# S5 lag table in DRAM with lags outside groups, its transfers on GpSimd's queue, output products issued strip by strip

## The chip, the cores and the metric

The kernel runs on one core of one Trainium2 chip, as one launch. The metric is the device time of the whole launch in microseconds (us). The engines that matter here: PE (TensorE, matrix products), PEld (its weight loads), DVE (VectorE), ACT (ScalarE), POOL (GpSimd) and SP (SyncE, which only issues DMAs). DMAs are issued from the queues of SP, ACT and POOL and are carried out by 16 DMA engines.

## The reference, cut to what matters

Two layers over 256 tokens of 2048 features: an S5 layer with its MLP, then a differential-attention layer with its MLP. The change touches the S5 mixer only. It has 128 groups of 16 features, and each group has 64 complex states:

```python
def s5_mixer(x, w_in, a_re, a_im, log_dt, b_re, b_im, c_re, c_im, d_skip, w_glu):
    u = (x @ w_in).reshape(Bsz, L, SSM_GROUPS, SSM_GROUP)
    step = exp(log_dt)[:, None]
    lam_re, lam_im = minimum(a_re, -1e-4), a_im
    abar = exp(step * lam_re) * (cos, sin)(step * lam_im)
    bbar = (abar - 1) / lam * b                       # complex
    # per group g: s_t = abar_g s_{t-1} + bbar_g u_t ;  y_t = Re(c_g s_t)
    y = y + d_skip * u
    z = gelu(y)
    val, gate = split(z @ w_glu)
    return val * sigmoid(gate)
```

Whatever way the recurrence is cut, y is a sum over earlier tokens of a 16x16 matrix that depends on the group and on the lag only, plus what a state carries over from further back.

## The kernel before, in words

**Chunks of eight tokens.** The 256 tokens are cut into 32 chunks of 8. Inside a chunk, y is a product with a Toeplitz operand built from the lags 0 to 7; what comes from earlier chunks goes through the states at the chunks' borders. The 128 groups are worked in 8 units of 16 groups (`unit(hh)`, called unit 0 to 7 here). A unit runs in four steps:

1. Lines 606 to 615: A (powers of abar) and B are loaded by POOL, DVE makes E from them (lines 609 to 612), and PE sums each chunk's input into the states (L615, bank `psw`).
2. Lines 621 to 648: cb is loaded by POOL, DVE makes F (lines 627 to 629), and PE makes the lag table (L634, bank `psk`). ACT copies it to K (L642), DVE adds d_skip on the diagonal (L643), and four DMAs write K to the scratch `k_scr` in DRAM (L645). Eight DMAs then read it back as M (L648), one for each token of a chunk: each lands on 16 partitions, shifted by one lag against the one ahead, which is how the table becomes the Toeplitz operand. Slots 0 to 6 of `k_scr` hold zeros, which line 537 writes at the start.
3. Lines 652 to 683: the states are transposed (L657), turned by tables that POOL loads (rt, L660), scanned over the chunks on DVE and written to ST (L682, L683).
4. Lines 685 to 699: the output products. For each of 16 groups PE multiplies Vh with M (L690) and adds ST times F (L691) in the same piece of the bank `psy`; then DVE transposes (L694) and ACT applies the GELU. Units 0 to 3 write z32, units 4 to 7 the tile xa.

PE's array is used there in column strips: a group's product has 32 output partitions, and `tile_position=(0, 32 * g4)` names one of four strips. Line 689 walks the groups in order, two for each strip.

**What stands beside the units.** Two matrix products give PE work that does not belong to a unit: x @ w_in (L581, 16 chunks of weights, 1 MB each, 16 products of 128x512 in the trace for each) and the first 10 chunks of w_glu (L210, 32 products of 128x256 in the trace for each), which need z32 of units 0 to 3. The string `ORDER` says in which order the program's text issues pieces of x @ w_in (W) and steps of the units (digits). The framework's scheduler then makes one fixed order for each engine out of it; each engine works through its order and waits wherever an operand is not there. The weights (`raw`) have two buffers, and SP issues their loads as the buffers come free.

**Queues.** SP issues the weights, and in the kernel before also K's writes and M's reads. POOL issues A, B, cb and rt. After the units come the rest of w_glu (L187, L188, with weights split in two parts by ACT and DVE at lines 137 and 138), the MLP, the attention layer and its MLP, which the change leaves alone.

In the order lists below, `mb` is a bank of PE's results for a unit, `gb` one of the weight products, and numbers in names only count tiles.

Of the kernel before, what the change touches and what calls it, by code (L numbers as in the profile page):

```python
# [42 lines left out]
def trunk(tc, io, stop=None):  # L43
# [47 lines left out]
    class Slots:  # L91
        """the pools that a kind of buffer is drawn from in turn"""
# [19 lines left out]
    fine = [0]  # so many of the next weight blocks are split in short steps  # L112

    pinned = []  # what the splits of the next weight blocks queue behind
# [31 lines left out]
    class Moving:  # L146
        """16 feature tiles of [x hi | x lo], kept as two tiles"""
# [17 lines left out]
    def gemm_b(jobs, x, kts, group=1, tail=1):  # L165
        """jobs: (lazy weight chunk, evacuation); each makes one tile of 128 output features x 256 tokens
        from weights hi/lo and [x hi | x lo]. The last jobs sum all three products in one half of the
        bank, the others keep hi*hi apart from the two cross products."""
# [23 lines left out]
    def added(acc, out, other=None):  # L192
        """out = what the bank holds (+ other)"""
# [24 lines left out]
    class SumSq:  # L218
        """sum of squares over all features: the last term joins on the tensor engine"""
# [23 lines left out]
    class SumSqPE:  # L243
        """the same, every term on the tensor engine, four column tiles side by side"""
# [22 lines left out]
    def rstd_of(sums):  # L267
        """1 / sqrt(sums * scale + eps)"""
        ps, scale = sums
        sd = tmp("n1", bufs=1, pool_=late["p"])  # L270
        S.activation(sd, ps, AF.Sqrt, bias=eps, scale=scale)
        r = tmp("rst", bufs=2, pool_=late["p"])
        V.reciprocal(r, sd)
        return r
# [9 lines left out]
    def finish(gpost, r):  # L284
        """out = h + rms(y)*gpost, where the tensor engine adds the first tiles"""
# [17 lines left out]
    def post_norm(ss, gpost, outs):  # L303
        """h += rms(y)*gpost ; then for every tile the next norms' inputs: outs = [(dst, gpre)]"""
# [18 lines left out]
    # ------------------------------------------------------------------ S5 layer  # L323
    def s5():
# [9 lines left out]
        k_scr = dr.tile([G, SG, 15, SG], F32, name="k_scr")  # L334
# [18 lines left out]
        # ---- x*g, with the first weights between its parts  # L353
# [17 lines left out]
        # ---- tables in [group, state]  # L371
# [26 lines left out]
        # sin/cos of th through the half angle  # L398
# [24 lines left out]
        # powers of abar: pw[:, delta, ri, n]  # L423
# [25 lines left out]
        # coef = (abar - 1) / lam, B = abar^delta * coef kept as (Br, -Bi, -Br)  # L449
# [32 lines left out]
        # u^8 (unit) and mag^8, doubled over both partition halves  # L482
# [26 lines left out]
        # chunk rotations e^{i phi c}  # L509
# [24 lines left out]
        # zero slots of the lag table, D on its diagonal  # L534
        zt = ps_.tile([P, SG * 7 * SG], F32, name="zt")
        V.memset(zt, 0.0)
        DMA.dma_start(k_scr[:, :, 0:7, :], zt.rearrange("g (p s q) -> g p s q", p=SG, q=SG))
# [8 lines left out]
        # ---- per 16 groups  # L546
# [47 lines left out]
        def unit(hh):  # L594
# [6 lines left out]
            for jj in range(2):  # L601
# [11 lines left out]
                for g in range(8):  # L613
# [24 lines left out]
            # lag table -> DRAM -> Toeplitz operand  # L638
            K = ut("K", [4, 8, SG], bufs=2)
            for c4 in range(4):  # L640
                q = slice(32 * c4, 32 * c4 + 16)
                S.copy(K[q], psk[q].rearrange("p (s d q) -> p s d q", s=4, q=SG))  # L642
                V.tensor_tensor(K[q, :, 0, :], K[q, :, 0, :], dskip[q, 4 * hh : 4 * hh + 4, :], op=ADD)  # L643
                k0 = k_scr[0, 0, 0, 0:1]
                DMA.dma_start(dview(k0, (g0 + c4) * 3840 + 7 * SG, [[240, 16], [4 * 3840, 4], [1, 128]]), K[q].rearrange("p s d q -> p s (d q)"))  # L645
            M = ut("M", [16, 8 * SG], bufs=2)
            for t_ in range(8):
                DMA.dma_start(M[16 * t_ : 16 * t_ + 16], dview(k_scr[0, 0, 0, 0:1], g0 * 3840 + t_ * SG, [[240, 16], [3840, 16], [1, 128]]))  # L648
# [492 lines left out]
```

## Time and profile before

| | us |
|---|---|
| median of 3 runs | 2409.82 |
| lowest, highest | 2400.21, 2413.78 |
| the profiled execution, its span from first to last instruction | 2406.2 |
| PE busy | 2274.4 (95% of the span) |
| DVE busy | 1567.2 |
| ACT busy | 1000.6 |
| POOL busy | 30.4 |

The page's slices of 60.2 us show where PE is not full: its first seven tenths read 7 7 5 7 6 8 9, all later ones 9 or 8. The S5 units lie in slices 2 to 6. For the profiled execution only its span is given, and no time around it.

### The profile page before, as it was taken

Reading aid. Unit: us, or ns where it says so; the run is one execution under the profiler, and the core shown is the slowest. Engines: PE = TensorE matmul, PEld = TensorE weight load, DVE = VectorE, ACT = ScalarE, POOL = GpSimd, SP = SyncE. Lnnn points to the kernel's source line nnn. Section 1 sums busy time; section 2 is a strip of 40 time slices with the busy share of each in tenths; the row PEclk is TensorE's granted clock in tenths of the full one; section 3 lists DMA queues with packets and bytes.
Section 4 is the critical chain, followed back from the end, with each engine's and each line's share of the span. In section 5 each row is a group of like instructions: output and inputs, shape, how many; then the busy total and the mean of one; then the engine's idle time right before and its main releaser. Section 6 shows DMA issues by size and latency. Waiting matters only on the chain.

```text
span 2406.2 us, 32521 instructions
## 1 busy us (share of the span) xinstructions
PE 2274.4 (95%) x13137; PEld 1903.0 (79%) x13137; DVE 1567.2 (65%) x2392; ACT 1000.6 (42%) x1470; POOL 30.4 (1%) x54
## 2 busy tenths in 40 slices
PE   7757689989999999999999999998999999999999
PEld 3335578868888888888868888886888888888887
DVE  8557656867556656656668896656765665665655
ACT  3011125554444444443554455444544444444442
POOL 0100100000000000000000000000000000000000
PEclk9878889999999999999999999999999999999999
DMA  9888976425554554554525544443555555555542
GB/s 282 198 167 159 165 172 248 174 97 210 201 202 173 197 191 174 197 190 158 206 99 188 180 171 162 158 175 123 189 197 210 181 187 192 183 186 192 186 165 104
DMA packets 93943, 432.25 MB, mean 180 GB/s; under 512 B 17377, under 2 KB 39649, under 8 KB 46433
## 3 DMA queue, kind: packets, MB, share of 16 engines
q1 hardware_dynamic: 82624, 405.51, 50.5%
q0 software_dynamic: 9984, 22.04, 4.8%
q10 hardware_dynamic: 1184, 2.62, 0.3%
q8 instruction: 103, 1.69, 0.3%
q14 instruction: 48, 0.39, 0.0%
HBM read 423.44 MB, written 6.68 MB: 179 GB/s over the span
## 4 chain that ended last, share of the span: by engine, by line
PE 85%; DMA 8%; DVE 4%; SPq 1%; ACT 1%; issue 1%; DVEq 0%; ACTq 0%
PE gb L187 47%; PE gb L188 24%; DMA M<-k_scr 4%; DMA raw<-in_w_in_dram 2%; PE gb L184 2%; PE gb L183 2%; PE gb L185 2%; PE mb L256 1%; PE gb L581 1%; DMA k_scr<-K 1%; PE gb L959 1%; PE gb L957 1%; PE gb L958 1%; SPq L648 1%; PE mb L690 1%
## 5 line engine op out<-in xcount | busy, mean ns | idle before, releaser
L138 DVE TENSOR_TENSOR wlo<-raw,whi 128x2048 fp32r<-128x2048 f32 (+1 forms) x540 | 803.1, 1506 | 509.8 <-ACT whi L137 507.6
L137 ACT CAST whi<-raw 128x2048 fp32r<-128x2048 f32 (+1 forms) x540 | 673.3, 1278 | 573.9 <-PE gb L187 375.1
L187 PE MATMUL gb<-x,whi 128*128 128x512 f32 x2400 | 848.8, 398 | 0.0
L188 PE MATMUL gb<-x,wlo 128*128 128x256 f32 x2400 | 675.1, 281 | 0.0
L187 PEld LDWEIGHTS gb<-x,whi 128*128 128x128 f32 x2400 | 450.6, 188 | 109.6
L187 PE MATMUL gb<-xa,whi 128*128 128x512 f32 x1296 | 465.2, 398 | 0.0
L188 PEld LDWEIGHTS gb<-x,wlo 128*128 128x128 f32 x2400 | 453.0, 189 | 0.2
L187 PE MATMUL gb<-xb,whi 128*128 128x512 f32 x1176 | 419.5, 395 | 0.4 <-ACT whi L137 0.4
L188 PE MATMUL gb<-xa,wlo 128*128 128x256 f32 x1296 | 367.8, 284 | 0.0
L188 PE MATMUL gb<-xb,wlo 128*128 128x256 f32 x1176 | 332.0, 283 | 1.6 <-DVE wlo L138 1.6
L187 PEld LDWEIGHTS gb<-xa,whi 128*128 128x128 f32 x1296 | 244.7, 189 | 61.9 <-issue 2.0
L187 PEld LDWEIGHTS gb<-xb,whi 128*128 128x128 f32 x1176 | 221.4, 188 | 52.8 <-issue 2.5
L188 PEld LDWEIGHTS gb<-xa,wlo 128*128 128x128 f32 x1296 | 245.7, 190 | 8.5 <-issue 8.2
L188 PEld LDWEIGHTS gb<-xb,wlo 128*128 128x128 f32 x1176 | 222.9, 190 | 5.2 <-issue 2.9
L215 ACT COPY cr<-gb 128x256 f32<-128x256 f32 x323 | 118.3, 368 | 169.1 <-PE gb L188 167.2
L581 PE MATMUL gb<-raw,h 128*128 128x512 f32 x256 | 122.3, 634 | 23.7 <-DMA raw<-in_w_in_dram 15.6
L162 ACT CAST x<-t 128x256 fp32r<-128x256 f32 x128 | 51.8, 406 | 198.9 <-DVE t L791 174.5
L581 PEld LDWEIGHTS gb<-raw,h 128*128 128x128 f32 x256 | 50.3, 202 | 88.3 <-issue 62.5
L690 PE MATMUL mb<-M,Vb 128*32 128x128 f32 x256 | 36.0, 338 | 76.0 <-DMA M<-k_scr 63.4
L200 DVE TENSOR_TENSOR t<-gb,cr 128x256 f32<-128x256 f32 x151 | 63.1, 418 | 54.9 <-ACT cr L215 54.5
L690 PEld LDWEIGHTS mb<-M,Vb 128*32 128x32 f32 x256 | 19.9, 130 | 82.1 <-issue 78.5
L210 PE MATMUL gb<-z,raw 128*128 128x256 f32 x320 | 72.3, 387 | 2.6 <-DMA raw<-in_w_glu_dram 2.6
(272 smaller groups left out, 2058.5 us busy)
## 6 DMA issues: line engine op xcount, KB each, us to landing
raw<-in_w_up_dram SPq DMA_DIRECT2D x128, 1024.0 KB, 4.7
raw<-in_w_down_dram SPq DMA_DIRECT2D x128, 1024.0 KB, 4.7
raw<-in_w_glu_dram SPq DMA_DIRECT2D x32, 1024.0 KB, 5.1
raw<-in_w_k_dram SPq DMA_DIRECT2D x16, 1024.0 KB, 4.7
raw<-in_w_q_dram SPq DMA_DIRECT2D x16, 1024.0 KB, 4.7
raw<-in_w_v_dram SPq DMA_DIRECT2D x16, 1024.0 KB, 4.7
raw<-in_w_o_dram SPq DMA_DIRECT2D x16, 1024.0 KB, 4.7
raw<-in_w_in_dram SPq DMA_DIRECT2D x15, 1024.0 KB, 10.8
```

What stands on the lines that cost most here:

```text
L137: S.copy(hi[:, c : c + n], raw[:, c : c + n])
L138: V.tensor_tensor(lo[:, c : c + n], raw[:, c : c + n], hi[:, c : c + n].bitcast(F32), op=SUB)
L162: mark[0] = S.copy(dst.hi(dt), src)
L183: T.matmul(ps[:, 0:L], hi[:, c], x.hi(kt), start=f, stop=False)
L184: T.matmul(ps[:, 0:L], hi[:, c], x.lo(kt), start=False, stop=False)
L187: T.matmul(ps, hi[:, c], x.both(kt), start=f, stop=False)
L188: T.matmul(ps[:, L : 2 * L], lo[:, c], x.hi(kt), start=False, stop=l)
L200: V.tensor_tensor(out, ps[:, 0:L], cr, op=ADD)
L210: T.matmul(ps[:, 0:L], w[:, off + kt * P : off + kt * P + P], x[:, kt, :], start=(kt == 0), stop=(kt == nk - 1))
L215: S.copy(cr, ps[:, L : 2 * L])
L581: T.matmul(pss[e], xg[:, kt, e * P : e * P + P], w[:, k4 * 512 : k4 * 512 + 512], start=(kt == 0), stop=(kt == 15))
L690: T.matmul(o, Vh[:, 8 * jj + g, :], M[:, 8 * jj + g, :], start=True, stop=False, tile_position=(0, 32 * g4))
```

## The change

`k_scr` is laid out anew. Before it was [group, feature, lag slot, feature], so that one group's 8 lags of a row are 512 bytes in one run. Now it is [unit, c4, feature, lag slot, 4 groups x 16 features]: four groups of a unit lie beside each other inside a lag, so that 8 lags of a row and four groups are 2 KB in one run. K and M take the matching shapes, and M is read by PE with a stride between lags. The zeros are written in 512 runs of 1792 bytes instead of 2048 of 448. K's writes and M's reads go out on POOL's queue instead of SP's. The input sums (L615) walk the strips 0, 1, 2, 3 in turn, and the output products come as four products with M, one for each strip, and then four with ST.

```diff
-        k_scr = dr.tile([G, SG, 15, SG], F32, name="k_scr")
+        k_scr = dr.tile([8, 4, SG, 15, 4 * SG], F32, name="k_scr")
...
-        zt = ps_.tile([P, SG * 7 * SG], F32, name="zt")
+        zt = ps_.tile([P, 4, 7 * 4 * SG], F32, name="zt")
         V.memset(zt, 0.0)
-        DMA.dma_start(k_scr[:, :, 0:7, :], zt.rearrange("g (p s q) -> g p s q", p=SG, q=SG))
+        DMA.dma_start(dview(k_scr[0, 0, 0, 0, 0:1], 0, [[4 * 960, P], [960, 4], [1, 448]]), zt)
...
-                for g in range(8):
+                for g in (0, 2, 4, 6, 1, 3, 5, 7):
                     g4, gh = g // 2, g % 2
...
-            K = ut("K", [4, 8, SG], bufs=2)
+            K = ut("K", [8, 4, SG], bufs=2)
+            k0 = k_scr[0, 0, 0, 0, 0:1]
             for c4 in range(4):
                 q = slice(32 * c4, 32 * c4 + 16)
-                S.copy(K[q], psk[q].rearrange("p (s d q) -> p s d q", s=4, q=SG))
-                V.tensor_tensor(K[q, :, 0, :], K[q, :, 0, :], dskip[q, 4 * hh : 4 * hh + 4, :], op=ADD)
-                k0 = k_scr[0, 0, 0, 0:1]
-                DMA.dma_start(dview(k0, (g0 + c4) * 3840 + 7 * SG, [[240, 16], [4 * 3840, 4], [1, 128]]), K[q].rearrange("p s d q -> p s (d q)"))
-            M = ut("M", [16, 8 * SG], bufs=2)
+                S.copy(K[q], psk[q].rearrange("p (s d q) -> p d s q", s=4, q=SG))
+                V.tensor_tensor(K[q, 0, :, :], K[q, 0, :, :], dskip[q, 4 * hh : 4 * hh + 4, :], op=ADD)
+                nc.gpsimd.dma_start(dview(k0, (4 * hh + c4) * 15360 + 448, [[960, 16], [1, 512]]), K[q].rearrange("p d s q -> p (d s q)"))
+            M = ut("M", [4, 8, 4, SG], bufs=2)
             for t_ in range(8):
-                DMA.dma_start(M[16 * t_ : 16 * t_ + 16], dview(k_scr[0, 0, 0, 0:1], g0 * 3840 + t_ * SG, [[240, 16], [3840, 16], [1, 128]]))
+                nc.gpsimd.dma_start(
+                    M[16 * t_ : 16 * t_ + 16].rearrange("p c t s q -> p c (t s q)"),
+                    dview(k0, 4 * hh * 15360 + t_ * 64, [[960, 16], [15360, 4], [1, 512]]),
+                )
...
             for jj in range(2):
-                for g in range(8):
-                    g4, gh = g // 2, g % 2
-                    o = psy[32 * g4 : 32 * g4 + 32, (2 * jj + gh) * P : (2 * jj + gh) * P + P]
-                    T.matmul(o, Vh[:, 8 * jj + g, :], M[:, 8 * jj + g, :], start=True, stop=False, tile_position=(0, 32 * g4))
-                    T.matmul(o, ST[:, jj, gh, g4, :], Fs[jj][:, g, 1:9, :].rearrange("p d q -> p (d q)"), start=False, stop=True, tile_position=(0, 32 * g4))
+                for gh in range(2):
+                    outs = [psy[32 * i : 32 * i + 32, (2 * jj + gh) * P : (2 * jj + gh) * P + P] for i in range(4)]
+                    for g4 in range(4):
+                        gl = 8 * jj + 2 * g4 + gh
+                        T.matmul(outs[g4], Vh[:, gl, :], M[:, gl % 4, :, gl // 4, :], start=True, stop=False, tile_position=(0, 32 * g4))
+                    for g4 in range(4):
+                        f = Fs[jj][:, 2 * g4 + gh, 1:9, :].rearrange("p d q -> p (d q)")
+                        T.matmul(outs[g4], ST[:, jj, gh, g4, :], f, start=False, stop=True, tile_position=(0, 32 * g4))
```

The scheduler makes another order out of this. On PE, at the last two units, the order before has unit 7's sums, lag table and transposes, then two chunks of w_glu (raw_1974, raw_1996), and then unit 7's output products, bank mb_1765:

```order
L615 MATMUL mb_1655<-E_1661,Vb_1283 32x128 x8
L615 MATMUL mb_1655<-E_1678,Vb_1283 32x128 x8
L634 MATMUL mb_1656<-F_1693,cb_1691 16x128 x8
L634 MATMUL mb_1656<-F_1706,cb_1691 16x128 x8
L657 MATMUL mb_1743<-ident,wsb_1741 128x128 x4
L210 MATMUL gb_1976<-z_406,raw_1974 128x256 x8
L210 MATMUL gb_1986<-z_406,raw_1974 128x256 x8
L210 MATMUL gb_1998<-z_406,raw_1996 128x256 x8
L210 MATMUL gb_2008<-z_406,raw_1996 128x256 x8
L690 MATMUL mb_1765<-M_1732,Vb_1283 32x128
```

The order of the change at the same place on PE:

```order
L615 MATMUL mb_1655<-E_1661,Vb_1283 32x128 x8
L615 MATMUL mb_1655<-E_1678,Vb_1283 32x128 x8
L634 MATMUL mb_1656<-F_1693,cb_1691 16x128 x8
L634 MATMUL mb_1656<-F_1706,cb_1691 16x128 x8
L660 MATMUL mb_1743<-ident,wsb_1741 128x128 x4
L694 MATMUL mb_1765<-M_1732,Vb_1283 32x128 x4
L697 MATMUL mb_1765<-F_1693,STt_413 32x128 x4
```

No weight product stands any more between unit 7's lag table and its output products; it is the same for unit 6, and all ten chunks of w_glu now stand ahead of unit 5's output products.

On PE, at unit 2 (bank mb_702 is its lag table, mb_991 its output), the order of the change:

```order
L634 MATMUL mb_702<-F_850,cb_848 16x128 x8
L634 MATMUL mb_702<-F_863,cb_848 16x128 x8
L660 MATMUL mb_900<-ident,wsb_898 128x128 x4
L615 MATMUL mb_945<-E_951,Vb_660 32x128 x8
L615 MATMUL mb_945<-E_968,Vb_660 32x128 x8
L210 MATMUL gb_1822<-z_406,raw_1820 128x256 x2
L210 MATMUL gb_1832<-z_406,raw_1820 128x256 x2
L210 MATMUL gb_1844<-z_406,raw_1842 128x256 x2
L210 MATMUL gb_1854<-z_406,raw_1842 128x256 x2
L694 MATMUL mb_991<-M_889,Vb_660 32x128 x4
```

Before, two whole chunks of w_in (raw_1167 and raw_1213) stood between unit 2's lag table and its output products; now it is two quarters of a w_glu chunk, and the w_in chunks have moved ahead of unit 1's output products. Unit 3 stands in the same way.

On POOL, at unit 4 (K_1251, M_1264), one piece of the difference:

```order
 L621 DMA cb_1540<-in_cb_dram 128x768
+L645 DMA k_scr<-K_1251 16x512 x4
 L606 DMA A_1506<-a_scr 128x1x1024
-L660 DMA rt_1597<-rot_scr 128x2x256
+L648 DMA M_1264<-k_scr 16x4x512 x8
 L607 DMA B_1507<-in_bE_dram 128x1x1024
 L606 DMA A_1523<-a_scr 128x1x1024
 L607 DMA B_1524<-in_bE_dram 128x1x1024
+L663 DMA rt_1597<-rot_scr 128x2x256
```

K's four writes and M's eight reads now stand on POOL between the loads for unit 6 (A_1506 to B_1524) and the tables for later units; on SP only weights are left.

Counted over the S5 part, weight chunks that PE works between a unit's lag table and its output products (w_in chunks for units 0 to 2 or 3, w_glu chunks for the later ones; a chunk of either takes PE about as long):

| unit | 0 | 1 | 2 | 3 | 4 | 5 | 6 | 7 | after 7 |
|---|---|---|---|---|---|---|---|---|---|
| before | 2.75 | 2 | 2 | 1.75 | 2.25 | 2 | 2 | 2 | 1 |
| change | 5 | 3.1 | 0.5 | 0.5 | 4.3 | 4.2 | 0 | 0 | 0 |

## Rows read from the trace of the kernel before

**Rows 1.** The page, part 1: busy us (share of the span), instructions.
```profile
PE 2274.4 (95%) x13137; PEld 1903.0 (79%) x13137; DVE 1567.2 (65%) x2392; ACT 1000.6 (42%) x1470; POOL 30.4 (1%) x54
```

**Rows 2.** Waits, 0 to 420 us: total us, times, longest.
```profile
PE mb L690 <- DMA M<-k_scr: 63.4, 6, 23.0
...
PE mb L690 <- issue: 11.6, 1, 11.6
```

**Rows 3.** PE in order of time: start us, us, what, [idle before <- releaser].
```profile
88.05 19.19 PE L581 MATMUL gb<-raw,h 128*128 128x512 f32 x44
119.27 0.60 PE L690 MATMUL mb<-M,Vb 128*32 128x128 f32 x2 [12.03 <-DMA M<-k_scr]
...
135.46 7.03 PE L581 MATMUL gb<-raw,h 128*128 128x512 f32 x16
...
173.87 0.61 PE L690 MATMUL mb<-M,Vb 128*32 128x128 f32 x2 [23.00 <-DMA M<-k_scr]
...
310.40 0.66 PE L657 MATMUL mb<-ident,wsb 128*128 128x128 f32 x4
...
328.52 0.60 PE L690 MATMUL mb<-M,Vb 128*32 128x128 f32 x2 [3.65 <-DMA M<-k_scr]
...
335.05 0.79 PE L615 MATMUL mb<-E,Vb 128*32 128x128 f32 x20
...
335.93 1.12 PE L634 MATMUL mb<-F,cb 128*16 128x128 f32 x23
337.37 0.65 PE L657 MATMUL mb<-ident,wsb 128*128 128x128 f32 x4 [0.32 <-ACT wsb L652]
337.86 13.98 PE L210 MATMUL gb<-z,raw 128*128 128x256 f32 x64
353.42 0.38 PE L690 MATMUL mb<-M,Vb 128*32 128x128 f32 x2 [1.58 <-DMA M<-k_scr]
...
357.65 7.17 PE L210 MATMUL gb<-z,raw 128*128 128x256 f32 x32
...
367.56 0.39 PE L188 MATMUL gb<-xb,wlo 128*128 128x256 f32 x1 [1.59 <-DVE wlo L138]
```

**Rows 4.** The chain that ended last, 0 to 420 us: start us, us, what.
```profile
151.66 21.88 DMA M<-k_scr
...
315.50 1.63 DMA k_scr<-K
...
340.81 1.60 DMA k_scr<-K
...
346.09 7.19 DMA M<-k_scr
```

**Rows 5.** Tile M: its reads on SP (ns min/median/max) and their landing.
```profile
L648 SPq DMA_DIRECT2D M<-k_scr x64: 302/448/2357, 94.1 to 346.1; - x64
...
DMA to landing us min/median/max: 3.0/7.4/21.9
```

**Rows 6.** Tile cb: its loads on POOL (ns min/median/max) and their landing.
```profile
L621 POOL DMA_DIRECT2D cb<-in_cb_dram x8: 557/578/616, 25.3 to 276.8; - x8
...
DMA to landing us min/median/max: 3.5/8.4/29.1
```

**Rows 7.** Tile A: its loads on POOL and their landing.
```profile
L606 POOL DMA_DIRECT2D A<-a_scr x16: 576/602/724, 22.9 to 291.4; - x16
...
DMA to landing us min/median/max: 6.4/15.0/28.2
```

**Rows 8.** DMA issues, 0 to 400 us: count, KB each, median us to landing.
```profile
raw<-in_w_glu_dram SPq DMA_DIRECT2D x22, 1024.0 KB, 7.4
raw<-in_w_in_dram SPq DMA_DIRECT2D x15, 1024.0 KB, 10.8
```

**Rows 9.** All engines in order of time, unit 6's last write to ST on DVE.
```profile
320.98 0.41 DVE L683 TENSOR_TENSOR STt<-t,t 64x248 f32<-64x248 f32 x1
```

**Rows 10.** One window: us, PE, PEld, DVE, ACT, POOL busy (count), PEclk, DMA share, GB/s.
```profile
160.00:200.00 40.00, 23.86 (x186) 14.47 (x188) 21.92 (x31) 4.13 (x7) 3.71 (x6) 0.79 1.00 170
```

## The prediction

> **What bounds the kernel now.** I read the busy times first: PE is busy 95% of the span [rows 1], so little is to be had outside the stretch where it is not full, the S5 units. There I read what PE waits for. The longest wait is for M, the lag table read back from DRAM: 63.4 us in six waits, and one of 11.6 us at the same line is put down to "issue" [rows 2]; together 75.0 us ahead of output products. In order of time the pattern is plain: PE works its weight chunks to 107.24 (88.05 + 19.19), then idles 12.0 us for unit 0's M, 23.0 for unit 1's, and at the end 3.7 for unit 6's and 1.6 for unit 7's [rows 3]. The chain says why: M's last read lands 21.9 us after its issue in unit 1 and 7.2 in unit 7 [rows 4]; over all 64 reads the landing is 3.0 at best, 7.4 in the middle [rows 5]. In 160 to 200 us the DMA engines are fully busy at only 170 GB/s, and PE's mean granted clock is 0.79: part of the stretch runs at 1.2 GHz instead of 2.4 [rows 10]. So the stage is bound by K's and M's trip through DRAM, unit after unit, less the weight chunks that PE has meanwhile.
>
> That trip, from the end of a unit's transposes (L657) to its first output product, is 15.4 us in unit 7 (338.02 to 353.42) and 17.5 in unit 6 (311.06 to 328.52) [rows 3], with two chunks of 7.0 us each as cover. The change shortens the trip, but it also takes the cover away from units 2, 3, 6 and 7 and gives it to units 0, 1, 4 and 5. The sum has to weigh both.
>
> **The change part by part.** I sum the stretch from 107.24, up to where both orders are nearly alike, to 367.56, where the split weight products run (L188). It lasts 260.3 us before. The order on PE behind it is the same.
>
> *Work that only moves.* Six w_in chunks at 7.03 are 42.2; ten w_glu chunks at 13.98 / 2 = 6.99 are 69.9 [rows 3]. A unit's sums, table and transposes take 3.0 (335.05 to 338.02) [rows 3]; what lies in the stretch, seven units less what runs inside a trip, is 19.9.
>
> *Strip by strip.* Unit 7's 64 output products take 4.2 us (353.42 to 357.65), 66 ns each, and unit 6's, after a wait, 6.5 (328.52 to 335.05) [rows 3]. No row shows products with M and ST alternating over strips. The nearest are the table's products, which change strips each time (1.12 / 23 = 49 ns), and the sums (0.79 / 20 = 40 ns) [rows 3]. I take 45 ns: 2.9 us at the full clock and 2.9 x 6.5 / 4.2 = 4.4 after a wait. Bounds: no gain at all, and 40 ns. M's strided read on PE has no row either; I take nothing for it, and the no-gain bound covers a loss. Four units with cover and four without: 4 x 2.9 + 4 x 4.4 = 29.2.
>
> *The trip.* In unit 7 K's last write is issued 2.8 us after the transposes (340.81) and lands after 1.6; eight reads follow, and the last lands 7.2 after its issue [rows 4]. On POOL's queue: 2.8 stays. The landing of a 32 KB write there has no row; it lies between 1.6 on SP's queue and 3.5, the quickest 384 KB load on POOL's [rows 6], and I take 2.3, nearer to the small transfer. An issue on POOL costs 0.58 [rows 6], so eight are 4.6. With a quarter of the runs and no weights loading beside it, the last 128 KB should land in the best time seen, 3.0 [rows 5]; the other bound is 7.2, as now. Sum 12.7. In unit 6 ACT and DVE have unit 5's results to handle first, and K's last write goes out 4.4 after the transposes (315.50) [rows 4]: 14.3. The trip can't be shorter than ST, which is written 10.3 after unit 6's transposes [rows 9, 3].
>
> *Waits for M afterwards.* Units 0, 1, 4, 5 have 5, 3.1, 4.3 and 4.2 chunks, about 22 us or more, and hide a trip even if a load of A stands ahead of M in POOL's queue (unit 4: M's eighth read waits for A_1506's semaphore, 15.0 us at the median [rows 7]). That cover is gone only if M needs over 22 us. Unit 2 has unit 3's sums and half a chunk, 4.5 us; unit 3 half a chunk, 3.5; units 6 and 7 nothing. Waits: 12.7 - 4.5 = 8.2, 12.7 - 3.5 = 9.2, 14.3 and 12.7, together 44.4, where it was 75.0.
>
> *What is late next: weights.* PE takes more chunks in a row, and two buffers allow one load ahead. With 10.8 us for a w_in load and 7.4 for a w_glu load [rows 8], each issued as the chunk two ahead is done: 3.9 at the first chunk (its buffer is free after 28 of the 44 products from 88.05 on, at 100.3 [rows 3]), 3.8 at the third, 3.8 at the fifth and sixth, 5.6 at the second w_glu chunk, a quarter of which stands ahead of unit 1's output, and 5.7 at the third, whose buffer is free only after unit 3. With 1.3 for E of unit 2, 24.1. Without K's and M's short runs on SP's queue loads may land sooner: if each takes 7.4, some 12 us of this go.
>
> *POOL's queue.* Twelve more issues a unit, 7 us, on an engine that is busy 30 us in all [rows 1]. Behind them wait the loads of A and B for later units and rt; DVE needs them only after the next output products, 15 us or more later, and I cost that at nothing; if that cover fails, E comes late by the excess. The zeros in longer runs and their place on SP's queue ahead of the first big loads lie before 107.24; nothing there waits for them by the rows, so nothing.
>
> *Tail.* From unit 7's last product to the split weights it is 9.9 us (357.65 to 367.56), of which a w_glu chunk fills 7.2 now [rows 3]. That chunk has moved ahead; the 9.9 stand bare.
>
> Sum: 42.2 + 69.9 + 19.9 + 29.2 + 44.4 + 24.1 + 9.9 = 239.6, against 260.3: a gain of 20.7 us. The profiled execution's span is 2406.2, nothing is given around it, and the median of the runs lies 3.6 higher. 2406.2 - 20.7 + 3.6 = 2389.
>
> **The rivals.** *Strips don't overlap*: products accumulating in one place, M then ST, keep 66 ns. For it speaks that today's order, where two neighbouring pairs also change strips, shows none of the sums' 40 ns. Units lose 1.3 and 2.1 each, 4 x 1.3 + 4 x 2.1 = 13.6: 2403.
>
> *The landing stays*: bytes, not runs, set it, and the last read lands after 7.2. Four bare trips grow by 4.2: 2406. Against it: fully busy DMA engines at 170 GB/s [rows 10] speak of costly short runs.
>
> *Cover lost, slower than before*: K and M queue behind A, B and cb on POOL's queue, where A's median landing is 15.0 [rows 7]. If the bare trips' reads land like that, each grows by 12.0: 48 us, 2437. It decides from a landing of 3.0 + 20.7 / 4 = 8.2 us on (no gain), and 11.2 makes it slower by over 0.5%. For it: units 2 and 3 have those loads near. Against it: units 6 and 7 have none ahead that is not long landed.
>
> *DVE holds up POOL's issues*: each of twelve issues waits for the DVE instruction that is running, 21.92 / 31 = 0.71 us [rows 10]. Four bare trips grow by 8.5: 34 us, 2423. Against it, the issues on POOL span only 557 to 616 and 576 to 724 ns [rows 6, 7] while DVE is busy over half the time. The Trainium skill has this as a rule against moving DMAs to that queue ("SBUF — State Buffer", SBUF: two separate sides): descriptors of GpSimd's DMAs can't be written while a DVE instruction in a two-port mode holds the shared port, and one took 3100 ns instead of 620. By that figure twelve issues could lose 30 us a unit, an estimate from that page of the Trainium skill; the trace's issues show no such case, so it stays at a small chance.
>
> The change may also fail to do what it says in the first place: the reads may not get cheaper (the landing rival) or the strips not overlap (the first).
>
> **How the numbers follow.** Forecast, with loads and trips somewhat better or worse: 0.66. Strips 0.11, landing 0.09, cover lost 0.10, DVE 0.04. On the good side, all loads at 7.4 give -12 (2377), and trips at ST's bound -11 (2366). The range 2366 to 2412 takes in the forecast, the strips and the landing, and leaves out cover lost, DVE and a little below. A measurement of this kernel can tell about 0.5%, 12 us: faster is below 2398, slower above 2422. Faster: the forecast and a third of the strips' case, 0.69. Same: the rest of the strips, the landing and a part of DVE, 0.18. Slower: 0.13.
>
> **What would show it.** In the profile after, waits for M before the output products of units 2, 3, 6 and 7 near 8, 9, 14 and 13 us and near none in the others; output products 2.9 us after cover and 4.4 after a wait; M's landing near 3; POOL's issues near 0.58; PE waiting for raw some 23 us behind 107; L188 running at 347. It is wrong if M's landing is above 8, if output products keep 4.2 and 6.5 us, if POOL's issues stretch, or if E or rt come late behind M on POOL's queue.

## The result, and the profile after

The changed kernel takes 2429.04 us (median of 5 runs, 2422.45 to 2434.44), the kernel before 2409.82 (2400.21 to 2415.60). The ratio is 1.0083, 95% interval 1.0058 to 1.0109: slower by 0.8%, 40 us above the forecast of 2389 and 17 us above the top of its range. The profiled execution has a span of 2427.3 us. The split weight products, up to which the prediction summed, start at 391.85 us instead of 367.56 [rows 3]; the loss of 24 us is all ahead of that point; behind it PE's work is the same and 3 us come back.

The page after, part 1, answers [rows 1]; the columns are the same.

```profile
PE 2262.6 (93%) x13137; PEld 1891.1 (78%) x13137; DVE 1566.9 (65%) x2392; ACT 1000.9 (41%) x1470; POOL 79.2 (3%) x150
```

PE has 12 us less work and a longer span: it waits more. For what, the waits of PE from 107 to 392 us say (total us, times, longest), which answer [rows 2]:

```profile
PE mb L694 <- DMA M<-k_scr: 57.1, 4, 19.1
PE gb L210 <- DMA raw<-in_w_glu_dram: 27.2, 5, 13.8
PE gb L581 <- DMA raw<-in_w_in_dram: 17.2, 2, 8.6
PE gb L187 <- ACT whi L137: 7.8, 2, 7.3
PE gb L210 <- ACT z L703: 3.6, 2, 2.7
```

The waits for M fell from 75.0 to 57.1 us, but four in place of seven, all in the bare units 2, 3, 6 and 7. New are 44.4 us of waits for weights, where there were 3.8, and a bare tail. PE in order of time, to be read against [rows 3] (start us, us, what, idle before and its releaser):

```profile
169.09 9.35 PE L581 MATMUL gb<-raw,h 128*128 128x512 f32 x16 [8.64 <-DMA raw<-in_w_in_dram]
...
193.93 3.71 PE L210 MATMUL gb<-z,raw 128*128 128x256 f32 x8 [13.76 <-DMA raw<-in_w_glu_dram]
...
217.34 0.65 PE L694 MATMUL mb<-M,Vb 128*32 128x128 f32 x8 [10.75 <-DMA M<-k_scr]
...
225.38 6.78 PE L210 MATMUL gb<-z,raw 128*128 128x256 f32 x16 [2.69 <-ACT z L703]
...
355.53 0.65 PE L694 MATMUL mb<-M,Vb 128*32 128x128 f32 x8 [19.06 <-DMA M<-k_scr]
...
361.96 0.66 PE L660 MATMUL mb<-ident,wsb 128*128 128x128 f32 x4
378.12 0.66 PE L694 MATMUL mb<-M,Vb 128*32 128x128 f32 x8 [15.51 <-DMA M<-k_scr]
...
389.02 1.22 PE L187 MATMUL gb<-xb,whi 128*128 128x512 f32 x2 [7.26 <-ACT whi L137]
```

The row at 225.38 also shows the clock: 16 products take 6.78 us where 64 took 13.98 in [rows 3], so each takes twice as long. The chip grants 1.2 instead of 2.4 GHz for part of the stretch, after PE has stood idle. Two windows of 40 us say how much of it (columns as in [rows 10]; the granted clock, PEclk, is the third from the end):

```profile
180.00:220.00 40.00, 14.61 (x209) 11.92 (x212) 21.47 (x32) 4.13 (x7) 9.70 (x19) 0.72 0.82 142
...
340.00:380.00 40.00, 8.96 (x168) 8.51 (x172) 23.64 (x41) 4.47 (x9) 11.95 (x24) 0.55 0.43 70
```

Unit 7's trip is bare: its transposes end at 362.62 and its first product runs at 378.12. POOL in order of time shows K's last writes, the wait for them and M's reads, and tile M's answer for 362 to 379 us the landing (from a DMA's issue until its data is there), which answers [rows 5]:

```profile
364.97 0.97 POOL L645 DMA_DIRECT2D k_scr<-K  x2 [0.20 <-DVE K L644]
367.85 4.07 POOL L648 DMA_DIRECT2D M<-k_scr  x8 [1.91 <-DMA k_scr<-K]
```
```profile
DMA to landing us min/median/max: 3.2/5.0/6.6
```

Reads cost 0.51 us each to issue (4.07 / 8) and the last lands 6.6 us after its issue, with nothing else loading. The same reads in unit 6, in windows of 2 us (DMA share and GB/s are the last two columns), show why:

```profile
348.00:350.00 2.00, 0.00 (x0) 0.00 (x0) 2.00 (x2) 0.00 (x0) 1.34 (x3) 0.50 1.05 135
350.00:352.00 2.00, 0.00 (x0) 0.00 (x0) 2.00 (x3) 0.00 (x0) 0.00 (x0) 0.50 1.03 135
```

The engines are fully busy at 135 GB/s with M alone. At that rate its megabyte takes 7.8 us, an estimate from these rows, however early each read is issued.

### The profile page after: what moved, and what is told of

Read it like the earlier page. It is cut to its first block, busy times and chain, and to the rows that moved or that the text cites. A ratio compares the mean times of both kernels' runs of the same rounds, so it can differ in the third digit from the quotient of the medians.

```text
span 2427.3 us, 32521 instructions
## 1 busy us (share of the span) xinstructions
PE 2262.6 (93%) x13137; PEld 1891.1 (78%) x13137; DVE 1566.9 (65%) x2392; ACT 1000.9 (41%) x1470; POOL 79.2 (3%) x150
## 4 chain that ended last, share of the span: by engine, by line
PE 84%; DMA 2%; issue 2%; DVE 2%; ACT 1%; POOL 1%; POOLq 0%; ACTq 0%
PE gb L187 47%; PE gb L188 24%; PE gb L210 2%; PE gb L184 2%; PE gb L183 2%; PE gb L185 2%; PE mb L256 1%; PE gb L965 1%; PE gb L964 1%; PE gb L963 1%; DMA raw<-in_w_glu_dram 1%; DMA M<-k_scr 1%; POOL M L648 0%; DVE wlo L138 0%; ACT whi L137 0%
## 5 line engine op out<-in xcount | busy, mean ns | idle before, releaser
L210 PE MATMUL gb<-z,raw 128*128 128x256 f32 x320 | 79.7, 412 | 30.8 <-DMA raw<-in_w_glu_dram 27.2
L210 PEld LDWEIGHTS gb<-z,raw 128*128 128x128 f32 x320 | 65.5, 208 | 44.0 <-issue 29.8
L163 DVE TENSOR_TENSOR x<-t,x 128x256 fp32r<-128x256 f32 x128 | 53.8, 422 | 30.3 <-ACT x L162 30.3
## 6 DMA issues: line engine op xcount, KB each, us to landing
raw<-in_w_in_dram SPq DMA_DIRECT2D x15, 1024.0 KB, 10.2
```

Of the source, the lines that this page charges most:

```text
L163: mark[1] = V.tensor_tensor(dst.lo(dt), src, dst.hi(dt).bitcast(F32), op=SUB)
L210: T.matmul(ps[:, 0:L], w[:, off + kt * P : off + kt * P + P], x[:, kt, :], start=(kt == 0), stop=(kt == nk - 1))
```

## The experiments

Names: the *parts* are the new table layout and the strips; the *queue* is where K's writes and M's reads are issued; the *order* is where PE's weight chunks stand. "Cover" is the chunks between a unit's transposes and its products. The shares below are differences of ratios to the kernel before, each good to some 0.3%.

### The parts and the queue, each alone

```diff
-                nc.gpsimd.dma_start(dview(k0, (4 * hh + c4) * 15360 + 448, [[960, 16], [1, 512]]), K[q].rearrange("p d s q -> p (d s q)"))
+                DMA.dma_start(dview(k0, (4 * hh + c4) * 15360 + 448, [[960, 16], [1, 512]]), K[q].rearrange("p d s q -> p (d s q)"))
...
-                nc.gpsimd.dma_start(
+                DMA.dma_start(
                     M[16 * t_ : 16 * t_ + 16].rearrange("p c t s q -> p c (t s q)"),
```

> The changed kernel with K's writes and M's reads back on SyncE's queue; the new table layout, the zeros in long runs and the strip-by-strip products stay. PE's order is then the one of before (cover of 2 chunks ahead of nearly every unit's products, two ahead of units 6 and 7). Theory COVER (the queue move loses because it lets PE's order put the weight chunks ahead of units 0, 1, 4 and 5 and leaves 2, 3, 6 and 7 bare): products fall from 4.2 to about 1.9 us after cover and from 6.5 to 3.5 after a wait, some 20 us over eight units, and M's landing of 7.2 in unit 7 falls by 1 to 3 us; time 2375 to 2395, and PE waits for M's reads under 70 us in all. Theory PARTS (the long-run layout with its strided operand, or the strips, cost something elsewhere that eats their gain): 2405 or more.

Measured: 2372.44 us, ratio 0.9857 (0.9827 to 0.9888), 3 us below COVER's range. **This version beats both kernels**, the changed one by 2.26% or 54 us. Its waits of PE from 100 to 400 us:

```profile
PE mb L694 <- DMA M<-k_scr: 56.5, 8, 12.7
PE mb L615 <- DVE E L612: 5.1, 1, 5.1
...
PE gb L581 <- DMA raw<-in_w_in_dram: 0.8, 1, 0.8
PE gb L210 <- DMA raw<-in_w_glu_dram: 0.7, 2, 0.4
```

PE waits as long for M as in the changed kernel, but hardly for weights: while PE waits for M, weights land, and while it works on them, M lands. The parts are sound; the queue, or what it does to the order, loses.

The kernel before with the queue alone (the same edit the other way, on the old lines):

> The kernel before with nothing but K's writes and M's reads moved to GpSimd's queue: old table layout with runs of 512 B, old order of the products. PE's order takes the shape of the changed kernel's (cover 5.5, 3.4, 0.5, 0.5, 4.3, 4.2, 0, 0 chunks). Theory COVER: this part alone makes it slower than both, since the products still take 4.2 to 6.5 us and the bare trips have the dearer short runs: 2440 to 2465. Theory PARTS (the loss sits in the layout or the strips): 2410 or less.

Measured: 2446.48 us, ratio 1.0163 (1.0130 to 1.0195), as expected. Its waits have the changed kernel's pattern, M late in the two bare units, rt in the two others, and weights late:

```profile
PE mb L690 <- DMA M<-k_scr: 34.0, 2, 17.4
PE mb L690 <- DMA rt<-rot_scr: 30.5, 2, 16.8
PE gb L210 <- DMA raw<-in_w_glu_dram: 29.4, 6, 11.9
PE gb L581 <- DMA raw<-in_w_in_dram: 13.7, 3, 10.4
```

Its bare trips are also a check on the run length. With 512 B runs M's last read lands 6.8 and 5.8 us after its issue in units 6 and 7, no later than with 2 KB runs (6.5 and 6.6 in the changed kernel), and the engines are as full with M alone (a window of 2 us in unit 6):

```profile
362.00:364.00 2.00, 0.00 (x0) 0.00 (x0) 2.00 (x3) 0.00 (x0) 0.00 (x0) 0.50 1.00 119
```

The kernel before with the strips alone, and with the layout alone (both as in the change, on SyncE's queue):

> The kernel before with nothing but the products (and the unit's sums) issued strip by strip. PE's order of units and chunks stays as before. Theory COVER: products take 1.9 us after cover and 3.5 after a wait instead of 4.2 and 6.5, and since the next unit's table is only summed after them, most of the 8 x 2.5 us stays: 2388 to 2398. Theory PARTS: what the products save comes back as a longer wait for the next M, 2405 to 2412.

> The kernel before with nothing but the new table layout (2 KB runs for M, the zeros in long runs), on SyncE's queue, with the old order of the products. PE's order of units and chunks as before. Theory ADD (the parts add up on SyncE's queue): both parts gave 34.2 us of span and the strips alone 11.5, so the layout gives 20 to 25: 2380 to 2388. Theory BYTES (bare reads of M move 135 GB/s with 2 KB runs and 123 with 512 B, so run length hardly matters): gain under 10 us, 2397 or more.

Measured: strips 2396.65 us, ratio 0.9953 (0.9940 to 0.9967); layout 2391.09 us, ratio 0.9926 (0.9909 to 0.9942). Together 1.2%, and both in one kernel 1.4%: they add up, as far as the intervals can tell. The layout alone lies 3 us above its range. Its gain sits above all in units 0 and 1, whose waits fell from 12.0 and 23.0 us [rows 3] to 4.2 and 12.4, and part of that comes back in unit 2 (the first output products there, before and with the layout alone):

```profile
198.54 0.38 PE L690 MATMUL mb<-M,Vb 128*32 128x128 f32 x2 [0.96 <-DVE E L612]
```
```profile
197.22 0.61 PE L693 MATMUL mb<-M,Vb 128*32 128x128 f32 x2 [13.29 <-DMA M<-k_scr]
```

### Order or queue

Here the weight products are queued on PE behind a unit's transposes (T) or last output product (O), which gives them the places of before, while K and M stay on GpSimd's queue (`hold_w` counts chunks of w_in, `hold_g` halves of chunks of w_glu; the second number of a pair is the unit):

```diff
+        hold_w = {10: ('O', 0), 11: ('T', 1), 12: ('T', 1), 13: ('T', 2), 14: ('T', 2), 15: ('T', 3)}
+        hold_g = {0: ('T', 3), 2: ('T', 4), 4: ('T', 4), 6: ('T', 5), 8: ('T', 5), 10: ('T', 6), 12: ('T', 6), 14: ('T', 7), 16: ('T', 7), 18: ('O', 7)}
...
+                    if 4 * b + kq in hold_w:
+                        es.enter_context(tc.issue_after(at[hold_w[4 * b + kq]].ins))
```

> The changed kernel, K and M on GpSimd's queue, but the weight products pinned behind the units' transposes and outputs, so that PE's order between 107 and 392 us is that of the kernel before (cover 2.9, 2, 2, 1.75, 2.25, 2, 2, 2 chunks). Theory COVER: bare trips go; units 6 and 7 wait 0 to 3 us for M instead of 19.1 and 15.5, units 2 and 3 0 to 3 instead of 10.8 and 11.8; the waits for weights after long runs of chunks go too; time 2375 to 2395. Theory RING (M is late because K and M stand in GpSimd's queue behind the 384 KB loads and pay its issues): waits for M stay over 40 us in all, above all in units 0 to 3, and the time is 2415 or more.

Measured: 2399.99 us, ratio 0.9970 (0.9951 to 0.9989), between the two theories. The order alone costs 1.0083 - 0.9970 = 1.13%, 27 us; the queue with the order held costs 0.9970 - 0.9857 = 1.13%, another 27. What either theory gave to itself is shared in halves. The waits of the pinned kernel (its product line is L704):

```profile
PE mb L704 <- DMA M<-k_scr: 43.7, 5, 13.8
PE mb L704 <- issue: 18.2, 2, 12.5
PE mb L704 <- DMA rt<-rot_scr: 14.7, 1, 14.7
```

Ahead of products they are 76.6 us, more than in the changed kernel, but the waits for weights are nearly gone (2.2 us, and 5.1 ahead of a w_in chunk that the profile puts down to issue), and so is the tail's. So what the new order costs shows as late weights and a bare tail, not as longer waits for M.

### K, M, and a third queue

With the order of before in all (pinned where it needs it): K's writes on SyncE's queue and M's reads on GpSimd's, the other way round, and both on ScalarE's.

> The changed kernel with PE's order pinned to that of before, as in the run with the pinned order, but K's writes on SyncE's queue; M's reads stay on GpSimd's. Theory K (K's small writes stand in GpSimd's ring behind 384 to 512 KB loads, and M can't be issued before they land): most of the 24 to 28 us between the pinned run and the run on SyncE's queue comes back: 2372 to 2382. Theory M (M's megabyte shares one ring with A, B, cb and rt): 2392 to 2402.

> The changed kernel with M's reads on SyncE's queue and K's writes on GpSimd's. PE's order is then that of before without a pin (cover 2.9, 2, 2, 1.75, 2.25, 2, 2, 2 chunks). Theory K: K's landing behind the big loads costs it most of the loss of the pinned run, 2392 to 2402. Theory M: 2370 to 2380.

> The changed kernel with K's writes and M's reads both on ScalarE's queue, with PE's order pinned to that of before. Neither the weights (SyncE's queue) nor A, B, cb and rt (GpSimd's) stand in the same ring. Theory RING (the place behind other loads in a ring is what costs): 2372 or less, units 0 and 1 wait under 15 us together. Theory ENGINES (the 16 DMA engines are full between 100 and 300 us whatever the queue): 2370 to 2380, waits for M much as in the run on SyncE's queue, 50 to 60 us. If twelve issues a unit on ScalarE delay its copies of K, wsb and z: 2385 or more.

Measured: M on GpSimd's queue 2396.39 us, ratio 0.9959 (0.9945 to 0.9973); K there 2384.16, ratio 0.9905 (0.9891 to 0.9920). So M's place costs 1.0% and K's 0.5%, and the two together (1.13%) are less than their sum. The first run lies in theory M's range, the second 4 us above it: M's place is the dearer, but K's part is not nothing. The reason that theory M gave, one ring shared with A, B, cb and rt, is not what unit 7 shows. With K and M on SyncE's queue the loads of weights are issued behind M (SP in order of time); the engines run at 129 GB/s with M and at 389 to 438 once it has landed (two windows of 2 us); and the landing follows:

```profile
313.84 4.04 SPq L648 DMA_DIRECT2D M<-k_scr  x8
317.99 5.59 SPq L122 DMA_DIRECT2D raw<-in_w_glu_dram  x2
```
```profile
319.00:321.00 2.00, 2.00 (x11) 1.77 (x10) 0.00 (x0) 0.37 (x1) 0.00 (x0) 1.00 1.09 129
...
323.00:325.00 2.00, 1.40 (x46) 1.24 (x49) 0.00 (x0) 0.37 (x1) 0.00 (x0) 1.00 0.96 389
```
```profile
DMA to landing us min/median/max: 2.9/4.8/6.2
```

With M on GpSimd's queue the weights, on the other queue, are moved beside it, while its own queue carries nothing else from 310 to 346 us (POOL, then SP in order of time, a window, the landing):

```profile
327.14 4.03 POOL L658 DMA_DIRECT2D M<-k_scr  x8 [19.10 <-DMA k_scr<-K]
```
```profile
329.26 7.26 SPq L122 DMA_DIRECT2D raw<-in_w_glu_dram  x2
```
```profile
334.00:336.00 2.00, 2.00 (x10) 1.52 (x9) 0.00 (x0) 0.00 (x0) 0.00 (x0) 1.00 0.97 250
```
```profile
DMA to landing us min/median/max: 3.2/6.3/9.8
```

M's last read lands 9.8 us after its issue instead of 6.2, and the trip is 18.3 us instead of 14.4. Other runs repeat it: in units 6 and 7 the last read lands after 5.8 to 7.0 us in the three runs with M on SyncE's queue (these parts, K alone moved, and the same without A and B, below), and after 9.4 to 9.8 in the three pinned ones with M on GpSimd's (this one, K there too, and that without A and B). A shared queue serves M first; two queues share the engines. The Trainium skill has this as a rule ("DMA: Bandwidth & Descriptors", Queues, rings and completion order): an engine goes in turn round the queues that have work for it, a packet at a time. The 6.2 and 9.8 us agree with it; the prediction did not weigh it.

On ScalarE's queue it is 2428.97 us, ratio 1.0092 (1.0077 to 1.0107): both theories missed, and the side remark came true. ScalarE's own work stands still behind M's reads: it is idle for 20.3 us in unit 4, where the reads wait some 7.6 us until K's last write has landed (8.6 us after its issue) and then take 12.7 us to be issued. Why the eight issues spread so far is not shown (ACT in order of time, unit 4):

```profile
252.63 12.72 ACTq L658 DMA_DIRECT2D M<-k_scr  x8
265.39 0.37 ACT L196 COPY h<-gb 128x256 f32<-128x256 f32 x1 [20.33 <-DMA M<-k_scr]
```

### What the waits are made of

A and B are loaded for the first half of unit 0 alone, so their traffic, their issues on GpSimd's queue and DVE's waits for them are left out together; with that, the changed kernel, the pinned one, and the one with K and M on SyncE's queue:

```diff
+                if gj == 0:
+                  nc.gpsimd.dma_start(A.rearrange("p g r n -> p (g r n)"), dview(a0, gj * P, [[G * P, 8], [0, 16], [1, 8 * P]]))
+                if gj == 0:
+                  nc.gpsimd.dma_start(B0.rearrange("p g r n -> p (g r n)"), dview(io["bE"], gj * P, [[0, 8], [G * P, 16], [1, 8 * P]]))
...
+                V.tensor_tensor(E, bc(A[:, :, 0, :], 2, 2), B0, op=MUL)
+                V.tensor_tensor(Bq, bc(A[:, :, 1, :], 2, 2), B0, op=MUL)
```

> The changed kernel, but A and B (512 KB each, twice a unit on GpSimd's queue) are loaded for the first half of unit 0 alone and used for all: fifteen sixteenths of their traffic is left out, so the E of the later groups is not the reference's. PE's order stays that of the changed kernel (cover 5.3, 3.5, 0.5, 0.5, 4.4, 4.1, 0, 0). Theory ENGINES (in units 0 to 5 M and the weights are late because the DMA engines are full, in units 6 and 7 because PE has no cover): waits for weights fall from 62 us to under 30, those for M in units 2 and 3 from 22.5 to 8 to 14, units 6 and 7 keep 19 and 15.5: 2375 to 2395. Theory LATENCY (each trip is a chain of fixed latencies, as the prediction had it): under 12 us of gain, 2417 or more.

> The same part left out (A and B loaded for the first half of unit 0 alone) in the kernel with PE's order pinned to that of before, K and M on GpSimd's queue. Theory ENGINES: with two chunks of cover ahead of nearly every unit and the engines free, trips shrink from 26 to 30 us to 16 to 20, and the waits for M from 76.6 us to under 35: 2340 to 2360, and 30 us or more below the changed kernel without A and B, since the lost cover costs as much as before. Theory LATENCY: within 12 us of the pinned run, 2388 or more.

> The same part left out (A and B loaded for the first half of unit 0 alone) in the kernel with K and M on SyncE's queue. Theory ENGINES: trips shrink to 14 to 17, waits for M from 56.5 to under 20: 2325 to 2345. If the queue's cost (28 us between the pinned run and the run on SyncE's queue) was A and B in GpSimd's ring, it is now under 8 us; if it was that M on GpSimd's ring shares the engines with the weights, which on SyncE's ring have to wait for M, 8 to 25 us stay.

Measured: 2374.45, 2346.90 and 2311.85 us; ratios 0.9858, 0.9744 and 0.9595, each with an interval of 0.4% to either side at most. The last is 13 us below its range. Latency alone is out. But the changed kernel gains differently from what was expected of it. Its waits of PE from 107 to 395 us without A and B:

```profile
PE mb L699 <- DMA M<-k_scr: 33.3, 2, 18.2
PE mb L699 <- DVE E L617: 11.4, 1, 11.4
PE mb L699 <- DMA rt<-rot_scr: 10.0, 1, 10.0
PE gb L210 <- DMA raw<-in_w_glu_dram: 9.5, 3, 4.8
...
PE gb L582 <- DMA raw<-in_w_in_dram: 1.5, 1, 1.5
```

The waits for weights fall from 44.4 to 12.9 us for the same chunks (the 11.0 shown, and 1.9 just ahead of this window; from 0 us on, as in the expectation, from 62.0 to 27.9): most of them came with A and B. The waits ahead of products stay, 54.7 for 57.1, in units 2 and 3 as well, where 8 to 14 us were expected and 21.4 remain: a bare trip lasts 15 to 18 us without that traffic, and 15.5 to 21 with it. In the pinned kernel the waits ahead of products fall from 76.6 to 48.6 us, where under 35 was expected. On SyncE's queue nearly all go. The waits for M, 56.5 us with A and B, are 19.0 without (17.2 from 107 us on, and 1.8 in unit 0 ahead of it):

```profile
PE mb L699 <- DMA M<-k_scr: 12.3, 4, 6.6
PE mb L699 <- issue: 4.9, 2, 2.5
```

There two chunks nearly cover a trip, and it is A's and B's traffic that makes it longer than its cover.

The differences stay: changed less pinned is 1.14% without A and B (1.13% with them), pinned less SyncE's queue 1.49% (1.13%). So what the queue costs is not the place behind A and B in GpSimd's ring.

### Four reads of M in place of eight

```diff
-            for t_ in range(8):
...
+            for c4 in range(4):
+                DMA.dma_start(
+                    M[:, c4].rearrange("p t s q -> p (t s q)"),
+                    dview(k0, (4 * hh + c4) * 15360, [[64, 8], [960, 16], [1, 512]]),
+                )
```

> The kernel with K and M on SyncE's queue, but M read in four transfers of 256 KB, one for each strip of the table and each over all 128 partitions, instead of eight of 128 KB over 16 partitions. A read then needs one K write alone, and PE's order spreads sums and chunks a little differently (about two chunks ahead of each unit's products). Theory ISSUES (eight issues of 0.43 us, one after another, and the wait for the last K write are part of the trip): trips shorten by 2 to 4 us where they are bare, and by as much where the engines are full: 2345 to 2368. Theory BYTES (a megabyte in 2 KB runs at some 130 GB/s sets it, whoever writes to which partitions): 2366 to 2378, and the engines still move 125 to 145 GB/s while M alone loads in unit 7.

Measured: 2406.08 us, ratio 0.9991 (0.9975 to 1.0006). Both missed. PE's order splits products, sums and chunks into pieces, and PE waits for M 65.6 us in 21 pieces from 100 to 400 us, for 56.5 in 8 with eight reads; the last such wait of unit 7 ends 11.2 us after M's first issue (342.76 to 353.99), with eight reads after 10.0 (313.84 to 323.79). What the changed order costs and what the four reads do are not separated here. Whether 128 partitions take M at a better rate than 16 stays open: the windows of that trip move 201 to 251 GB/s, but M and weights together.

### Weights held back behind M

The pinned kernel on GpSimd's queue, with a write of 1 KB of M on SyncE's queue, which has to wait for M; the weight loads issued behind it wait too. In the second two of the four kernels (the lower part of the diff) the weight loads with these numbers are also put behind the write of the unit named:

```diff
+            dmp[hh] = DMA.dma_start(dump[hh], M[:, 3, 7, 3, 14:16])
...
+        late_w, late_g = {10: 0, 13: 1, 15: 2}, {1: 3, 3: 4, 5: 5, 7: 6, 9: 7}
```

> The kernel with the pinned order, K and M on GpSimd's queue, and one small transfer a unit added on SyncE's queue that writes 1 KB of M back to DRAM: it waits for M's last read, and the weight loads behind it on SyncE's queue wait with it, as they stand behind M where M is on that queue. Theory SHARING (on GpSimd's ring M loses to weight loads that run beside it from the other ring): M's last read lands 6 to 7.5 us after its issue in units 6 and 7 instead of 8.0 to 9.8, the waits for M fall from 76.6 us to under 65, 2375 to 2392. Theory FIFO (M and K stand behind A, B, cb and rt in their own ring): waits in units 0 to 5 stay, and since the weights come later the time is 2398 or more.

> The same small transfer that holds the weight loads back until M has landed, in the pinned kernel without A and B (loaded for the first half of unit 0 alone). Here only weights, cb and rt run beside M. Theory SHARING: most of the 35 us between that kernel and the one on SyncE's queue without A and B comes back: 2315 to 2332, waits for M under 25 us instead of 43. Rival LATER WEIGHTS: holding them back costs PE as much as M gains: 2340 or more, and PE waits for weights over 10 us.

Measured: 2399.47 and 2349.29 us, no different from the kernels without the write. It tells nothing on sharing: in units 6 and 7 two loads of weights were still issued while M's reads were, and the last read landed after 8.7 to 9.1 us.

> As the run that held the weights with one small transfer a unit, but the loads that were still issued beside M's reads (one pair a unit) are now queued behind that transfer too: SyncE's queue has the order of the kernel with K and M on it, with the small transfer in M's place. Theory SHARING: M's last read lands 6 to 7.5 us after its issue in units 6 and 7, their trips are 15 to 17.5 us instead of 18.2 to 20.3, and the time 2372 to 2390. Theory FIFO (A, B, cb and rt ahead in GpSimd's ring): trips of units 1 to 5 stay near 26, and with later weights the time is 2397 or more.

> The same queue of weights behind M without A and B (loaded for the first half of unit 0 alone). Theory SHARING: 2315 to 2335, M's last read lands under 7.5 us after its issue. Rival: M's landing falls but the weights come so late that PE waits for them, 2340 or more.

Measured: 2396.94 us, ratio 0.9963 (0.9949 to 0.9976), and 2336.76, ratio 0.9720 (0.9704 to 0.9737). The local part of SHARING came true: in units 6 and 7 M's last read lands at most 6.7 us after its issue in the first kernel and 6.5 in the second, unit 7's trip is 15.9 us in the first, and PE waits little ahead of products. But the weights now come late instead, as the first kernel's landing and its waits from 107 to 395 us say:

```profile
DMA to landing us min/median/max: 3.2/4.8/6.7
```
```profile
PE gb L598 <- DMA raw<-in_w_in_dram: 39.4, 3, 16.4
PE gb L213 <- DMA raw<-in_w_glu_dram: 27.0, 3, 12.2
PE mb L712 <- DMA B<-in_bE_dram: 13.4, 2, 7.8
PE mb L712 <- DMA M<-k_scr: 6.7, 2, 4.6
```

The total of SHARING missed in both; the first lies on the bound that FIFO gave (2397), the second between the two theories, so the totals decide nothing. A load that waits for M's landing starts some 6 us later, by the landings above, than one that is queued behind M's reads, and stands behind the small write besides. Shown is that weights beside M delay M; that this is the whole of the queue's 27 us is not.

## Why the prediction was wrong

The sum of the prediction, term by term, against the changed kernel from 108.43 (the end of the same chunk) to 391.85 us, from PE in order of time:

| term | forecast us | measured us |
|---|---|---|
| w_in and w_glu chunks | 112.1 | 126.3 |
| sums, tables, transposes | 19.9 | 20.0 |
| output products | 29.2 | 20.9 |
| waits for M | 44.4 | 57.1 |
| waits for weights, E and copies | 24.1 | 49.1 |
| tail | 9.9 | 10.1 |
| sum | 239.6 | 283.5 |

**Strips: right, and undersized.** 64 products take 1.8 us after cover (137.01 to 138.78) and 3.4 after a wait (217.34 to 220.73), for 2.9 and 4.4. At the full clock one takes 28 ns, less than the 45 that I took between the table's products and the sums. The first rival fell; the term is 8 us better.

**Moved cover: right.** PE waits for M in units 2, 3, 6 and 7 alone, and the tail stands bare, as forecast. This was the right thing to look for, and the pinned run prices the order at 27 us, though in late weights and the tail rather than in waits for M. The failing steps are the next three, which sized what follows from it.

**M's landing: the step that failed first.** I took 3.0 us, the best of 64 reads, for the last of eight. The best was a first read; the last waits for the megabyte ahead of it. Bare it lands after 6.4 to 6.6 us in all four units, nearly the 7.2 of before: the rival that the landing stays, which I gave 0.09, describes this term. Unit 7's trip is 15.5 us instead of 12.7, unit 6's 19.1 instead of 14.3, units 2 and 3 wait 2.5 more each: 12.7 us in all. Not all of it is M: each trip gets 1.0 us back at the issues, and K's landing was too short as well, from K's last issue to M's first 3.9 us in unit 6 and 5.9 in unit 3 where I had 2.3. [rows 10] had the sign of it, engines full at 170 GB/s; I read that as a price of 512 B runs, but with 2 KB runs they are full at 135, and the queue-only run, with 512 B, shows 117 to 129 in bare units.

**Weights: the largest miss.** I let PE take more chunks in a row and costed loads by their medians [rows 8], 10.8 and 7.4 us. But a bunched order asks for the weights when A, B, M and rt fill the engines. The loads behind the three longest of these waits, 8.5, 8.6 and 13.8 us, landed 15.3 to 15.4 us after their issue. 44.4 us of waits, 12.9 without A and B. "Loads may land sooner" was true of the medians, 10.2 and 7.0 us, and no help to these.

**Clock: a term that I left out.** I read a granted clock of 0.79 off [rows 10] and still costed the chunks at 7.03 and 6.99 us, durations at 2.4 GHz. After idle time they run in part at 1.2 GHz (granted clock 0.72 in the window from 180 us): 14.2 us, where the kernel before lost 2.6 by the same count.

**POOL's queue.** Issues span 512 to 535 ns for M's reads and 484 to 530 for K's writes, on an engine busy 79 us: the rival with DVE fell. The Trainium skill's rule on the shared port ("SBUF — State Buffer", SBUF: two separate sides) shows in no issue here, with DVE busy for much of the time; whether an instruction of the kind that the rule names ran beside them, no run here shows. A load of A did stand ahead of M's eighth read in units 0 and 4, for 3.6 and 5.4 us, and the cover hid it as forecast. What I costed at nothing, the move of K and M to a queue beside that of the weights, is worth 27 us with the order held; that weights beside M delay it is a part of that, how large a part is open. The rival on the slower side named the right end (2437) with half its mechanism: cover is lost, but the bare trips land at 6.6, below the 8.2 from which it was to decide; the time came from late weights, from a landing of 6.4 to 6.6 where I had 3.0, and from the clock. I gave this side 0.13.

## What to carry to other kernels

When a transfer moves to another queue, it loses its rank against what stays: on one queue M went ahead of the weights behind it, on two it shares the engines with them, and a scheduler no longer held by the queue's order moved the weight products too. Cost the last of a batch of transfers by the bytes ahead of it at the rate of the nearest full window, not by the best landing of one. Of a change in several parts, the parts that only make work cheaper (strips, longer runs) are worth having without the one that moves work: here they alone give 1.4%.

## What the runs showed of the hardware that I had not expected

- The 16 DMA engines are full at 127 to 139 GB/s with M's reads alone in 2 KB runs (changed kernel, units 6 and 7), at 117 to 129 with 512 B runs (queue-only run), and at 389 to 438 GB/s with weight loads of 8 KB a partition (the parts on SyncE's queue). Four times longer runs bring less than a tenth.
- The queue decides what a batch loses to loads beside it: M's last read lands after 5.8 to 7.0 us with the weights behind it on one queue and after 9.4 to 9.8 with them on another.
- Two accumulating products on each of four strips, issued strip by strip, take 28 ns each at 2.4 GHz, against 66 ns in the old order [rows 3].
